# Gate and up projections: products of a block summed by TensorE onto running PSUM banks

## The chip, the cores and the metric

The kernel runs on one core of a Trainium2 chip. That core has TensorE for matrix products (PE in the profile, with its weight loads as PEld), VectorE (DVE), ScalarE (ACT), GpSimd (POOL) and the DMA queues, here those that SyncE (SP) and GpSimd issue. Each engine takes its own instructions in order and waits for others through semaphores. The metric is the time of one execution on the device in microseconds (us). Three executions of the kernel before took 2392.41, 2394.06 and 2399.23 us; their median, 2394.06 us, is the time before.

## The reference

One encoder block on a sequence of 1024 rows of width 1024, all in float32:

```
x <- LN1(alpha*x + 0.5*FFN1(x))
x <- LN2(alpha*x + W_out [attention(x) ; RG-LRU(x)])
x <- LN3(alpha*x + 0.5*FFN2(x))
swiglu(x) = (silu(x @ w_gate) * (x @ w_up)) @ w_down      # the FFN: 1024 -> 4096 -> 1024
```

Only the two products `x @ w_gate` and `x @ w_up` of both FFNs are touched by the change. Attention, the recurrence, the layer norms and `w_down` stay as they are.

## The kernel before

**Precision.** Every float32 operand is split in two parts, hi (a cast by ScalarE) and lo (the rest, a subtraction by VectorE). A float32 product is then three matmuls, hi*hi + hi*lo + lo*hi (`mm3`, L149 to L155), each with a 128x128 weight tile and 512 columns.

**Seven products for eight.** Gate and up are computed in a Strassen-Winograd scheme. `gate_up` (L276) goes over 16 pairs of 128 hidden columns; in each pair it handles two matrices, gate and up. For each matrix there are four blocks of weights (`11`, `12`, `21`, `22`; differences `t1` to `t4` of them are made by VectorE in `less`, L299) and, made once for an FFN, eight operand blocks of x (`11`, `12`, `22`, `s1` to `s4`). Seven products of 12 matmuls each (`one` to `seven`, L341 to L362) are summed to the four 128x512 results `c[0]` to `c[3]`. Each product gets a fresh PSUM bank of the eight (`banks`, L80); ScalarE copies `one` and `five` to rows `p1` and `p5`, and VectorE does all the sums: one for `two`, two for `six`, one for `three`, two for `seven`, one for `four`, seven for a matrix and each 128x512. Then ScalarE applies silu to gate, and VectorE multiplies, forms sums for the down projection and GpSimd stores the result (`finish`, L417).

**The start of an FFN.** The operand blocks of x are made while pair 0 runs. `blocks_2` (L252) transposes the rows by TensorE into PSUM, and for each of four row blocks j it makes `s1` and `22`, then, after products `one` and `two`, `s2`, `s3` and `s4`: VectorE forms the difference (L268, L270, L272), ScalarE casts hi (L244), and lo is subtracted at L245, by VectorE for `s1`, `22` and `s2`, by GpSimd for `s3` and `s4` (L271, L273). Product `six` needs `s2` of all four row blocks, so TensorE can go on with `six` only when the fourth `s2` is there. In pair 0 the products run in the order one, two, five, four, six, three, seven for gate and up in turn.

**What sets the order.** The code is written in the order above, and a scheduler in the tile framework then places each instruction on its engine's queue; tiles and pools set the waits. Weight tiles `ws` are a ring of 16, raw weights `raw` a ring of two loads of 1 MB, rows `row` a ring of eight.

**After gate and up.** `down_ffn` (L438) multiplies the stored hidden blocks with `w_down`: its operands are cast by ScalarE at L465 and subtracted by VectorE at L466, from the first matmul on. Before the second FFN stands the attention, whose last rows pass through a layer norm (L194, L204).

Of the kernel before, what the change touches and what calls it, by code (L numbers as in the profile page):

```python
# [17 lines left out]
P = 128  # L18
# [33 lines left out]
class Block:  # L52
# [26 lines left out]
    @contextmanager  # L79
    def banks(self):  # L80
        with self.pool("bank", 8, space=PSUM) as ps:
            yield lambda: ps.tile([P, H], F32, tag="b", name=self.nm("b"))
# [66 lines left out]
    def mm3(self, out, lhs, rhs, first, last):  # L149

        mm = self.nc.tensor.matmul
        (ah, al), (bh, bl) = lhs, rhs
        mm(out, ah, bh, start=first, stop=False)  # L153
        mm(out, ah, bl, start=False, stop=False)  # L154
        mm(out, al, bh, start=False, stop=last)  # L155
# [86 lines left out]
    def block_parts(self, name, j, src, eng=None):  # L242
# [9 lines left out]
    def blocks_2(self, rows, bank, tmp):  # L252
# [13 lines left out]
        for j in range(4):  # L266
# [4 lines left out]
            self.block_parts("s3", j, t21[j], nc.gpsimd)  # L271
            v.tensor_tensor(s[j], a12, s[j], ALU.subtract)  # L272
            self.block_parts("s4", j, s[j], nc.gpsimd)  # L273
            yield

    def gate_up(self, wg, wu, h_d, rows, bank, tp, wsp, aside=None):  # L276
# [9 lines left out]
        def weights(pair, n, w):  # L286
# [18 lines left out]
            if pair == 0:  # L305
                w["21"] = parts(b21)
            yield
            t1 = less(b12, b11)
            w["t1"] = parts(t1)
            if pair == 0:  # L310
                t2 = less(b22, t1)
                w["t4"] = parts(less(b21, t2))
                yield
                w["t2"] = parts(t2)
            else:
                t2 = less(b22, t1)
                w["t2"] = parts(t2)
            yield
            w["22"] = parts(b22)
            yield  # L320
            w["t3"] = parts(less(b22, b12))
            yield
            if pair:
                w["21"] = parts(b21)
                w["t4"] = parts(less(b21, t2))

        class Matrix:


            def __init__(m):  # L330
                m.w = {}
                p = self.row()
                m.p1, m.p5 = p[:, 0:H], p[:, H:]

            def product(m, n, a):
                x = bank()
                for k in range(4):
                    self.mm3(x, tuple(t[:, k, :] for t in m.w[n]), tuple(t[:, k, :] for t in A[a]), k == 0, k == 3)
                return x

            def one(m):  # L341
                nc.scalar.copy(m.p1, m.product("11", "11"))

            def two(m):
                v.tensor_tensor(m.c[0], m.product("21", "12"), m.p1, ALU.add)
# [685 lines left out]
```

## Time and profile before

| what | value |
|---|---|
| median of three executions | 2394.06 us |
| the profiled execution's own time | 2396.48 us |
| its span in the trace | 2394.8 us, so 1.7 us lie around it |
| mean granted clock of TensorE | 0.985 of full speed |
| busy in the span | PE 97%, DVE 76%, ACT 41%, POOL 16% |
| gate and up of FFN1 and of FFN2 | about 17 to 646 us and 1433 to 2064 us |

The trace is one execution. Times in its rows are us from the start of the span; the granted clock is the share of TensorE's full 2.4 GHz that the chip gave, and 0.50 is its lower level, 1.2 GHz. A busy PE is not a PE at its peak; its matmuls overlap, so the time of one in a row is longer than the step from one to the next. The same overlap, smaller, is there on VectorE and ScalarE.

### The profile page before, as it was taken

Reading aid. Unit: us, or ns where it says so; the run is one execution under the profiler, and the core shown is the slowest. Engines: PE = TensorE matmul, PEld = TensorE weight load, DVE = VectorE, ACT = ScalarE, POOL = GpSimd, SP = SyncE. Lnnn points to the kernel's source line nnn. Section 1 sums busy time; section 2 is a strip of 40 time slices with the busy share of each in tenths; the row PEclk is TensorE's granted clock in tenths of the full one; section 3 lists DMA queues with packets and bytes.
Section 4 is the critical chain, followed back from the end, with each engine's and each line's share of the span. In section 5 each row is a group of like instructions: output and inputs, shape, how many; then the busy total and the mean of one; then the engine's idle time right before and its main releaser. Section 6 shows DMA issues by size and latency. Waiting matters only on the chain.

```text
span 2394.8 us, 29276 instructions
## 1 busy us (share of the span) xinstructions
PE 2318.7 (97%) x10709; PEld 1927.6 (80%) x10709; DVE 1814.8 (76%) x3059; ACT 993.3 (41%) x1748; POOL 383.0 (16%) x461
## 2 busy tenths in 40 slices
PE   7999999999999998999999898999999999999996
PEld 5888888888888886788888777888888888888885
DVE  7877777777667878866667889776777777568879
ACT  5343333333344444544546755333333333344443
POOL 2020000000000006311134542000000000010015
PEclk8999999999999999999999998999999999999998
DMA  3333233332374442333365812332323233555342
GB/s 129 116 96 115 84 118 101 111 106 93 137 257 160 158 159 71 87 105 95 106 185 141 238 53 75 110 115 84 115 89 127 94 105 115 189 213 186 125 145 88
DMA packets 175775, 298.99 MB, mean 125 GB/s; under 512 B 8128, under 2 KB 100608, under 8 KB 175632
## 3 DMA queue, kind: packets, MB, share of 16 engines
q1 hardware_dynamic: 151984, 216.06, 28.2%
q0 software_dynamic: 23648, 81.07, 9.0%
q8 instruction: 85, 1.39, 0.3%
q14 instruction: 58, 0.48, 0.1%
HBM read 214.22 MB, written 82.87 MB: 124 GB/s over the span
## 4 chain that ended last, share of the span: by engine, by line
PE 85%; DVE 8%; issue 3%; DMA 1%; ACT 1%; POOL 1%; SPq 0%; POOLq 0%; DVEq 0%; ACTq 0%
PE b L154 17%; PE b L155 17%; PE b L153 17%; PE s L155 5%; PE s L154 5%; PE s L153 5%; PE a L155 5%; PE a L154 5%; PE a L153 5%; DVE ws L466 2%; DVE row L194 2%; PE a L851 1%; DMA raw<-in_ffn_w_gate_dram 1%; DVE st L190 1%; PE a L835 1%
## 5 line engine op out<-in xcount | busy, mean ns | idle before, releaser
L153 PE MATMUL b<-As,ws 128*128 128x512 f32 x1024 | 400.7, 392 | 8.2 <-ACT As L244 8.2
L154 PE MATMUL b<-As,ws 128*128 128x512 f32 x1024 | 400.7, 391 | 3.8 <-DVE As L245 3.8
L155 PE MATMUL b<-As,ws 128*128 128x512 f32 x1024 | 400.3, 391 | 0.0
L153 PE MATMUL b<-A,ws 128*128 128x512 f32 x768 | 299.7, 390 | 4.3 <-ACT ws L295 4.3
L154 PE MATMUL b<-A,ws 128*128 128x512 f32 x768 | 299.2, 390 | 0.0
L155 PE MATMUL b<-A,ws 128*128 128x512 f32 x768 | 299.0, 389 | 0.0
L295 ACT CAST ws<-t 128x512 fp32r<-128x512 f32 x256 | 159.5, 623 | 331.0 <-PE b L154 304.3
L465 ACT CAST ws<-raw 128x512 fp32r<-128x512 f32 x224 | 139.2, 622 | 314.8 <-PE a L155 141.3
L466 DVE TENSOR_TENSOR ws<-raw,ws 128x512 fp32r<-128x512 f32 x224 | 167.8, 749 | 120.4 <-ACT ws L465 120.2
L153 PEld LDWEIGHTS b<-As,ws 128*128 128x128 f32 x1024 | 193.3, 189 | 48.7 <-ACT As L244 8.6
L154 PEld LDWEIGHTS b<-As,ws 128*128 128x128 f32 x1024 | 193.5, 189 | 45.4 <-DVE As L245 5.2
L155 PEld LDWEIGHTS b<-As,ws 128*128 128x128 f32 x1024 | 193.5, 189 | 40.2
L295 ACT CAST ws<-raw 128x512 fp32r<-128x512 f32 x192 | 119.2, 622 | 252.1 <-PE b L154 244.5
L296 DVE TENSOR_TENSOR ws<-t,ws 128x512 fp32r<-128x512 f32 x256 | 177.9, 695 | 53.2 <-ACT ws L295 53.1
L154 PE MATMUL a<-ws,ws 128*128 128x512 f32 x512 | 202.0, 395 | 7.0 <-DVE ws L466 6.9
L153 PE MATMUL a<-ws,ws 128*128 128x512 f32 x512 | 201.4, 394 | 1.4 <-ACT ws L465 1.3
L155 PE MATMUL a<-ws,ws 128*128 128x512 f32 x512 | 201.5, 394 | 0.0
L153 PEld LDWEIGHTS b<-A,ws 128*128 128x128 f32 x768 | 144.3, 188 | 34.3 <-ACT ws L295 4.7
L296 DVE TENSOR_TENSOR ws<-raw,ws 128x512 fp32r<-128x512 f32 x192 | 136.9, 714 | 44.7 <-ACT ws L295 44.6
L429 POOL DMA_DIRECT2D h_d<-row x32 | 18.6, 581 | 937.7 <-DVE row L421 906.2
L155 PEld LDWEIGHTS b<-A,ws 128*128 128x128 f32 x768 | 144.3, 188 | 29.9
L154 PEld LDWEIGHTS b<-A,ws 128*128 128x128 f32 x768 | 144.3, 188 | 29.7
(224 smaller groups left out, 4688.7 us busy)
## 6 DMA issues: line engine op xcount, KB each, us to landing
raw<-h_d SPq DMA_DIRECT2D x56, 1024.0 KB, 5.5
h_d<-row POOLq DMA_DIRECT2D x96, 512.0 KB, 3.4
raw<-in_ffn_w_gate_dram SPq DMA_DIRECT2D x32, 1024.0 KB, 5.5
raw<-in_ffn_w_up_dram SPq DMA_DIRECT2D x32, 1024.0 KB, 5.5
wd<-in_ffn_w_down_dram SPq DMA_DIRECT2D x32, 1024.0 KB, 7.8
h_d<-row POOLq DMA_DIRECT2D x32, 256.0 KB, 4.5
raw<-in_w_in_dram SPq DMA_DIRECT2D x16, 512.0 KB, 5.2
row<-in_x_dram SPq DMA_DIRECT2D x12, 512.0 KB, 7.5
```

Of the source, the lines that this page charges most:

```text
L153: mm(out, ah, bh, start=first, stop=False)
L154: mm(out, ah, bl, start=False, stop=False)
L155: mm(out, al, bh, start=False, stop=last)
L190: v.bn_stats(st[:, j, :], a[:, j * H:(j + 1) * H])
L194: v.scalar_tensor_tensor(a, a, mv[:, 0:1], gb[0], op0=ALU.subtract, op1=ALU.mult)
L295: nc.scalar.copy(hi, src)
L296: v.tensor_tensor(lo, src, f32(hi), ALU.subtract)
L429: return nc.gpsimd.dma_start(d[:, 6], s5)
L465: nc.scalar.copy(hi, src)
L466: self.mark = v.tensor_tensor(lo, src, f32(hi), ALU.subtract)
L835: nc.tensor.transpose(pa[:, (j % 4) * P:(j % 4 + 1) * P], p[:, j * P:(j + 1) * P], self.ident)
L851: mm(pv[:, ps], vt[:, j, :], pts[h, qt][j // 4][l][:, j % 4, ps], start=j == 0 and l == 0, stop=j == last and l == 1)
```

## The change

Two of the eight PSUM banks become a pool of their own for running sums. Product `one` opens a sum bank; `six`, `seven` and `four` are added onto it by TensorE itself, and between them the bank's state is copied out: by ScalarE after `one` (`s1`) and `six` (`u`), by VectorE with the addition of `s5` after `seven` (`c[3]`), by ScalarE after `four` (`c[2]`). Product `three` is added the same way onto the bank of `five`. VectorE keeps three sums of a matrix (`two`, `seven`, `three`). `four` of a matrix is put after `one` of the next matrix (`pending`). In pair 0 each matrix keeps five sums, and `three` comes last. `s3` and `s4` get their lo part from VectorE, as the others do. The weight parts are made in the order in which the products take them. The products with silu and the multiplication work on whole rows of 1024 in place of halves.

```diff
     def banks(self):
-        with self.pool("bank", 8, space=PSUM) as ps:
+        with self.pool("bank", 6, space=PSUM) as ps, self.pool("sum", 2, space=PSUM) as xs:
+            self.sum_bank = lambda: xs.tile([P, H], F32, tag="x", name=self.nm("x"))
             yield lambda: ps.tile([P, H], F32, tag="b", name=self.nm("b"))
...
-        (eng or self.nc.vector).tensor_tensor(lo, src, f32(hi), ALU.subtract)
+        self.nc.vector.tensor_tensor(lo, src, f32(hi), ALU.subtract)
...
-            self.block_parts("s3", j, t21[j], nc.gpsimd)
+            self.block_parts("s3", j, t21[j])
             v.tensor_tensor(s[j], a12, s[j], ALU.subtract)
-            self.block_parts("s4", j, s[j], nc.gpsimd)
+            self.block_parts("s4", j, s[j])
...
             w["11"] = parts(b11)
-            if pair == 0:
-                w["21"] = parts(b21)
+            w["21"] = parts(b21)
             yield
             t1 = less(b12, b11)
-            w["t1"] = parts(t1)
             if pair == 0:
+                w["t1"] = parts(t1)
                 t2 = less(b22, t1)
                 w["t4"] = parts(less(b21, t2))
                 yield
                 w["t2"] = parts(t2)
+                yield
+                w["t3"] = parts(less(b22, b12))
+                yield
+                w["22"] = parts(b22)
             else:
                 t2 = less(b22, t1)
                 w["t2"] = parts(t2)
...
+                w["t1"] = parts(t1)
+                w["t3"] = parts(less(b22, b12))
+                w["22"] = parts(b22)
                 w["t4"] = parts(less(b21, t2))
...
-            def product(m, n, a):
-                x = bank()
+            def product(m, n, a, x=None):
+                new = x is None
+                if new:
+                    x = bank()
                 for k in range(4):
-                    self.mm3(x, tuple(t[:, k, :] for t in m.w[n]), tuple(t[:, k, :] for t in A[a]), k == 0, k == 3)
+                    self.mm3(x, tuple(t[:, k, :] for t in m.w[n]), tuple(t[:, k, :] for t in A[a]), new and k == 0, k == 3, not new)
                 return x
 
             def one(m):
-                nc.scalar.copy(m.p1, m.product("11", "11"))
+                m.sum = self.sum_bank()
...
+                nc.scalar.copy(m.s1, m.sum)
...
+            def six(m):
+                nc.scalar.copy(m.u, m.product("t2", "s2", m.sum))
 
             def five(m):
-                nc.scalar.copy(m.p5, m.product("t1", "s1"))
-
-            def six(m):
-                v.tensor_tensor(m.u, m.product("t2", "s2"), m.p1, ALU.add)
-                v.tensor_tensor(m.c[1], m.u, m.p5, ALU.add)
+                m.z = m.product("t1", "s1")
+                nc.scalar.copy(m.s5, m.z)
+
+            def seven(m):
+                v.tensor_tensor(m.c[3], m.product("t3", "s3", m.sum), m.s5, ALU.add)
 
             def three(m):
-                v.tensor_tensor(m.c[1], m.product("22", "s4"), m.c[1], ALU.add)
-
-            def seven(m):
-                v.tensor_tensor(m.u, m.product("t3", "s3"), m.u, ALU.add)
-                v.tensor_tensor(m.c[3], m.u, m.p5, ALU.add)
+                v.tensor_tensor(m.c[1], m.product("22", "s4", m.z), m.u, ALU.add)
 
             def four(m):
-                v.tensor_tensor(m.c[2], m.product("t4", "22"), m.u, ALU.add)
+                nc.scalar.copy(m.c[2], m.product("t4", "22", m.sum))
...
-                for step in ("five", "four_alone", "six", "three", "seven_four"):
+                for step in ("five", "four_alone", "six_five", "seven_four", "three_alone"):
...
-                for m in (gate, up):
-                    for step in ("one", "two", "five", "six", "three", "seven", "four"):
-                        getattr(m, step)()
-                    if m is gate:
-                        silu(gate.c)
...
+            for m in (gate, up):
+                m.one()
+                if pending:
+                    pending()
+                for step in ("two", "six", "five", "seven", "three"):
+                    getattr(m, step)()
+
+                def pending(m=m, gate=gate, g=(g0, g1), end=end, last=pair == FF // P // 2 - 1):
+                    m.four()
                     if m is gate:
-                        silu(gate.c)
+                        silu(g)
+                    elif not last:
+                        end()
+        pending()
```

The line numbers of the changed kernel are higher by 2 in this part (L245 becomes L247, L268 becomes L270, L272 becomes L274, L296 becomes L298) and by 22 in `down_ffn` (L465 becomes L487, L466 becomes L488).

**VectorE while `s2`, `s3` and `s4` of FFN1 are made.** The stretch before, from the difference for the second row block to that for the third; `As2`, `As3`, `As4` are the operand blocks, `ws` here also holds the differences, `b` are banks, `t` differences of weights.

```order
L268 TENSOR_TENSOR ws_58_251<-ws_58_251,b_90_421 128x512
L270 TENSOR_TENSOR ws_57_250<-b_90_421,ws_57_250 128x512
L296 TENSOR_TENSOR ws_95_445<-t_81_352,ws_94_444 128x512
L245 TENSOR_TENSOR As2_18_118<-ws_58_251,As2_17_117 128x4x128
L296 TENSOR_TENSOR ws_103_515<-raw_42_198,ws_102_514 128x512
L272 TENSOR_TENSOR ws_58_251<-b_91_426,ws_58_251 128x512
```

The same stretch now:

```order
L270 TENSOR_TENSOR ws_60_255<-ws_60_255,b_92_425 128x512
L272 TENSOR_TENSOR ws_59_254<-b_92_425,ws_59_254 128x512
L247 TENSOR_TENSOR As4_15_117<-ws_56_237,As4_14_116 128x4x128
L247 TENSOR_TENSOR As2_19_121<-ws_60_255,As2_18_120 128x4x128
L247 TENSOR_TENSOR As3_13_115<-ws_59_254,As3_12_114 128x4x128
L274 TENSOR_TENSOR ws_60_255<-b_93_430,ws_60_255 128x512
L298 TENSOR_TENSOR ws_95_445<-t_76_342,ws_94_444 128x512
```

The subtractions for `As3` and `As4` now stand among VectorE's, and the splits of raw weights (`raw`) have moved behind the fourth `As2`. From the first of the four differences to the fourth `As2` VectorE has 22 instructions before and 23 now in FFN1, 20 before and 22 now in FFN2.

**TensorE where FFN2 begins.** Before: the end of product `one` of gate, then the transposes of the last rows that the layer norm delivers (`row`).

```order
L153 MATMUL b_2282_12640<-A1_2237_12426,ws_2273_12622 128x512
L154 MATMUL b_2282_12640<-A1_2238_12427,ws_2273_12622 128x512
L155 MATMUL b_2282_12640<-A1_2237_12426,ws_2274_12623 128x512
L239 MATMUL b_2285_12656<-ident_73,row_1086_5578 128x128 x4
L239 MATMUL b_2286_12662<-ident_73,row_1086_5578 128x128 x4
```

Now:

```order
L157 MATMUL x_2132_12369<-A1_2085_12151,ws_2124_12352 128x512
L155 MATMUL x_2150_12469<-A1_2085_12151,ws_2128_12361 128x512
L156 MATMUL x_2150_12469<-A1_2086_12152,ws_2128_12361 128x512
L157 MATMUL x_2150_12469<-A1_2085_12151,ws_2129_12362 128x512
L155 MATMUL x_2150_12469<-A1_2085_12151,ws_2128_12361 128x512
L156 MATMUL x_2150_12469<-A1_2086_12152,ws_2128_12361 128x512
L157 MATMUL x_2150_12469<-A1_2085_12151,ws_2129_12362 128x512
L241 MATMUL b_2135_12385<-ident_73,row_934_5303 128x128 x4
```

Six matmuls of `one` of up (`x_2150`, its sum bank) have moved in front of the transposes.

**ScalarE where gate and up of FFN1 end.** Before: the last copy (`five` of up), a small cast for a later stage, and then the casts of the down projection.

```order
L342 COPY row_968_4913<-b_1015_5095 128x512
L465 CAST ws_1038_5237<-raw_1030_5225 128x512
L348 COPY row_968_4913<-b_1017_5123 128x512
L138 CAST hi_1451_7814<-gate_raw_1284 128x256
L465 CAST ws_1039_5240<-wd_1031_5227 128x512
```

Now:

```order
L354 COPY row_822_4627<-x_867_4812 128x512
L358 COPY row_823_4628<-b_869_4868 128x512
L367 COPY row_823_4628<-x_867_4812 128x512
L140 CAST hi_1299_7539<-gate_raw_1338 128x256
L487 CAST ws_887_4967<-wd_879_4954 128x512
```

The copy at L367 takes `four` of up, the very last product, and the casts of `w_down` stand behind it. On VectorE the sum of the last product (L362), which stood in front of L466, is gone.

## Rows read from the trace of the kernel before

**Rows 1.** The page: busy time, share and instructions of each engine.

```profile
PE 2318.7 (97%) x10709; PEld 1927.6 (80%) x10709; DVE 1814.8 (76%) x3059; ACT 993.3 (41%) x1748; POOL 383.0 (16%) x461
```

**Rows 2.** Busy time by stretch: length, PE, PEld, DVE, ACT, POOL, clock, DMA.

```profile
240.00:300.00 60.00, 60.00 (x267) 49.67 (x266) 43.16 (x69) 21.00 (x35) 2.71 (x4) 1.00 0.25 84
...
1260.00:1320.00 60.00, 59.22 (x367) 52.17 (x366) 47.50 (x127) 40.30 (x97) 25.52 (x48) 1.00 0.59 153
```

**Rows 3.** Timeline of PE, FFN1: start, time, instruction, idle before.

```profile
53.53 1.22 PE L153 MATMUL b<-As,ws 128*128 128x512 f32 x2 [4.91 <-ACT As L244]
56.51 0.79 PE L154 MATMUL b<-As,ws 128*128 128x512 f32 x1 [1.75 <-DVE As L245]
...
62.57 0.40 PE L154 MATMUL b<-As,ws 128*128 128x512 f32 x1
```

**Rows 4.** Timeline of DVE, FFN1.

```profile
37.44 0.68 DVE L268 TENSOR_TENSOR ws<-ws,b 128x512 f32<-128x512 f32 x1
38.04 0.68 DVE L270 TENSOR_TENSOR ws<-b,ws 128x512 f32<-128x512 f32 x1
...
42.24 1.67 DVE L296 TENSOR_TENSOR ws<-t,ws 128x512 fp32r<-128x512 f32 x1
...
54.71 1.75 DVE L245 TENSOR_TENSOR As<-ws,As 128x512 fp32r<-128x512 f32 x1
```

**Rows 5.** Timeline of POOL, FFN1.

```profile
42.07 1.30 POOL L245 TENSOR_TENSOR As<-ws,As 128x512 fp32r<-128x512 f32 x1 [0.40 <-ACT As L244]
```

**Rows 6.** Timeline of PE, start of FFN2.

```profile
1435.63 0.39 PE L155 MATMUL b<-A,ws 128*128 128x512 f32 x1
1439.68 6.22 PE L239 MATMUL b<-ident,row 128*128 128x128 f32 x32 [3.66 <-DVE row L204]
1445.66 0.48 PE L153 MATMUL b<-A,ws 128*128 128x512 f32 x1
...
1467.52 1.03 PE L239 MATMUL b<-ident,row 128*128 128x128 f32 x8
1471.83 0.95 PE L153 MATMUL b<-As,ws 128*128 128x512 f32 x2 [3.27 <-ACT As L244]
1474.81 0.79 PE L154 MATMUL b<-As,ws 128*128 128x512 f32 x1 [2.03 <-DVE As L245]
...
1479.37 0.39 PE L154 MATMUL b<-As,ws 128*128 128x512 f32 x1
```

**Rows 7.** Timeline of DVE, start of FFN2.

```profile
1457.90 0.68 DVE L268 TENSOR_TENSOR ws<-ws,b 128x512 f32<-128x512 f32 x1
...
1473.01 1.75 DVE L245 TENSOR_TENSOR As<-ws,As 128x512 fp32r<-128x512 f32 x1
```

**Rows 8.** Stretches as in group 2, where the clock was low.

```profile
52.90:63.10 10.20, 7.81 (x19) 5.71 (x20) 9.14 (x11) 3.54 (x6) 4.55 (x3) 0.53 0.66 205
1438.70:1445.50 6.80, 5.82 (x30) 5.82 (x31) 5.13 (x8) 3.23 (x7) 0.53 (x1) 0.55 0.30 119
1472.85:1479.70 6.85, 4.89 (x13) 3.90 (x14) 6.06 (x8) 2.24 (x4) 2.92 (x2) 0.55 0.74 248
```

**Rows 9.** Timeline of PE where the down projections begin, FFN1 and FFN2.

```profile
646.48 1.45 PE L153 MATMUL a<-ws,ws 128*128 128x512 f32 x4
648.03 0.50 PE L154 MATMUL a<-ws,ws 128*128 128x512 f32 x1
...
2065.49 0.50 PE L154 MATMUL a<-ws,ws 128*128 128x512 f32 x1 [1.16 <-DVE ws L466]
```

**Rows 10.** Timeline of DVE, end of gate and up in FFN2.

```profile
2064.14 0.69 DVE L362 TENSOR_TENSOR row<-b,row 128x512 f32<-128x512 f32 x1 [0.83 <-PE b L155]
```

**Rows 11.** Timeline of ACT, end of gate and up in FFN1.

```profile
635.80 0.59 ACT L348 COPY row<-b 128x512 f32<-128x512 f32 x1 [2.10 <-PE b L155]
...
641.31 0.62 ACT L465 CAST ws<-wd 128x512 fp32r<-128x512 f32 x1 [4.62 <-DMA wd<-in_ffn_w_down_dram]
```

**Rows 12.** The page: DMA issues, count, KB each, us to landing.

```profile
raw<-in_ffn_w_gate_dram SPq DMA_DIRECT2D x32, 1024.0 KB, 5.5
```

More of the change, by code (lines that the diff above doesn't have):

```diff
@@ L147, in split_ws, with mm3 @@
         return hi, lo
-    def mm3(self, out, lhs, rhs, first, last):
+    def mm3(self, out, lhs, rhs, first, last, goes_on=False):
         mm = self.nc.tensor.matmul
         (ah, al), (bh, bl) = lhs, rhs
-        mm(out, ah, bh, start=first, stop=False)
-        mm(out, ah, bl, start=False, stop=False)
-        mm(out, al, bh, start=False, stop=last)
+        mm(out, ah, bh, start=first, stop=False, skip_group_check=goes_on)
+        mm(out, ah, bl, start=False, stop=False, skip_group_check=goes_on)
+        mm(out, al, bh, start=False, stop=last, skip_group_check=goes_on)
     def open_xT(self, pool, half):
@@ L339, in product @@
                 return x
             def one(m):
-                nc.scalar.copy(m.p1, m.product("11", "11"))
+                m.sum = self.sum_bank()
+                for k in range(4):
+                    self.mm3(m.sum, tuple(t[:, k, :] for t in m.w["11"]), tuple(t[:, k, :] for t in A["11"]), k == 0, k == 3)
+                nc.scalar.copy(m.s1, m.sum)
             def two(m):
-                v.tensor_tensor(m.c[0], m.product("21", "12"), m.p1, ALU.add)
+                v.tensor_tensor(m.c[0], m.product("21", "12"), m.s1, ALU.add)
@@ L364, in four_alone, with six_five, three_alone @@
             def four_alone(m):
                 nc.scalar.copy(m.c[2], m.product("t4", "22"))
+            def six_five(m):
+                m.six()
+                v.tensor_tensor(m.c[1], m.u, m.s5, ALU.add)
             def seven_four(m):
                 m.seven()
-                v.tensor_tensor(m.c[2], m.c[2], m.u, ALU.add)
+                v.tensor_tensor(m.c[2], m.c[2], m.sum, ALU.add)
+            def three_alone(m):
+                v.tensor_tensor(m.c[1], m.product("22", "s4"), m.c[1], ALU.add)
@@ L373, in silu, with halves @@
                 nc.scalar.activation(t, t, AF.Silu)
+        def halves(r):
+            return r[:, 0:H], r[:, H:]
+        pending = None
         for pair in range(FF // P // 2):
             if pair == 0:
[L377 to L385 removed]
@@ L386, in gate_up @@
-            h = h0, h1
-            gate.u, up.u = us
-            gate.c = [g[:, k * H:(k + 1) * H] for g in (g0, g1) for k in range(2)]
-            up.c = [h[n][:, m * H:(m + 1) * H] for m in range(2) for n in range(2)]
-            w = [weights(pair, n, m.w) for n, m in enumerate((gate, up))]
+                g0, h0, first, fifth, uu, g1, h1, u = (self.row() for _ in range(8))
+                homes = list(zip(halves(first), halves(uu), halves(fifth)))
+                gate, up = Matrix((g0, g1), *homes[0]), Matrix((h0, h1), *homes[1])
+            else:
+                g0, g1, uu, h0, h1, u = (self.row() for _ in range(6))
+                gate, up = (Matrix(r, r[1][:, 0:H], x, r[0][:, H:]) for r, x in zip(((g0, g1), (h0, h1)), halves(uu)))
@@ L391, in gate_up, with end @@
+            def end(pair=pair, finish=finish):
+                store = finish()
+                if aside is not None and pair == 2:
+                    with self.tc.issue_after(store.ins):
+                        aside()
             if pair == 0:
```

66 lines of the change are left out of this document (24 added, 42 removed).

## The prediction

> **What bounds the kernel now.** I read the page's busy shares first. VectorE is at 76%, so a change that takes sums from it looks promising; but TensorE is at 97% [rows 1]. The next view is the busy time by stretch. In the middle of gate and up TensorE is busy for the whole 60 us, issues 267 matmuls, one every 0.225 us, and holds the full clock [rows 2]; VectorE has 17 us to spare in that stretch and ScalarE 39. The stretches from 120 to 600 us and from 1500 to 2040 us read alike. There nothing but fewer matmuls could help, and the change leaves their number as it is. The reader should look for time only where TensorE stands still: the start of each FFN, and the step to the down projection.
>
> The timeline of TensorE shows the start of FFN1. After the transposes it waits 4.91 us for ScalarE's cast of the fourth `s2`, issues two matmuls, and waits 1.75 us more for VectorE's subtraction of it [rows 3]. So the chain is VectorE's, from the first difference at 37.44 us to the subtraction that starts at 54.71 and takes 1.75 [rows 4]: 19.02 us for 22 instructions. Undisturbed, VectorE starts the next instruction 0.60 us after the last, with 0.68 us for one [rows 4]; 22 would take 13.3 us. The missing 5.7 us sit in instructions like the one at 42.24 us, which takes 1.67 us while GpSimd's subtraction for `s3` or `s4` runs beside it for 1.30 us [rows 4, 5]; six of the 22 are stretched so. After the wait TensorE's clock is low: the mean is 0.53 of full speed from 52.9 to 63.1 us [rows 8].
>
> FFN2 begins with a wait of 3.66 us for the layer norm's last row, then 32 transposes at 0.55 of the clock, then the same two waits for the fourth `s2`, of 3.27 and 2.03 us, and again 0.55 of the clock [rows 6, 8].
>
> **The change part by part.**
>
> *Sums on TensorE's banks, from pair 1 on.* VectorE loses four sums in each of 30 matrices of an FFN, 240 in all, and half of its multiplications become double ones; at 0.60 us a sum that is 144 us of VectorE's time. ScalarE gets two more copies a matrix, 120 of about 0.59 us [rows 11], 71 us. TensorE issues the same 12 matmuls a product, 12 x 0.225 = 2.7 us. I take 0 for all of it, since TensorE is the engine that never waits here [rows 2]. What is new is that `six`, `seven`, `four` and `three` wait for the copy of their bank. The copy starts close behind the product's end and takes 0.59 us [rows 11], and a whole product of 2.7 us lies between: about 1.9 us in hand. If the cover goes, each microsecond of lateness is a microsecond of TensorE's (a rival, below).
>
> *`s3` and `s4` without GpSimd.* In FFN1 VectorE now has 23 instructions from the first difference to the fourth `As2`, of which six are subtractions that GpSimd did; the two splits of raw weights that stood among them come later. With GpSimd silent I price all at the undisturbed step: 22 x 0.60 + 0.68 = 13.9 us, against 19.0, so -5.1. In FFN2 the chain runs from 1457.90 to 1473.01 + 1.75, 16.9 us for 20 instructions [rows 7]; 22 now take 21 x 0.60 + 0.68 = 13.3, so -3.6. Bounds: nothing gained, if the stretching has another cause; and no more than the waits that there are, 6.7 us in FFN1 and 5.3 in FFN2 [rows 3, 6]. So 1.6 to 1.7 us of waiting should stay in each. The Trainium skill (Perfetto Trace Analysis, Optimizing Scalar/DVE Operations) speaks against this edit on one side: where VectorE is saturated, as it is in these 19 us, handing work to ScalarE or even GpSimd may make sense. The same passage adds that GpSimd and VectorE share a read port into SBUF, so that it may not help. By the first half the chains would grow by the instructions added and the sum would lose its two largest terms; the instruction that takes 1.67 us beside GpSimd's speaks for the second half.
>
> *The clock in the ramps.* From 56.51 to 62.57 us TensorE issued 14 matmuls [rows 3], 6.06 us where 14 x 0.225 = 3.15 are enough: 2.9 us. From 1474.81 to 1479.37 it issued 11 [rows 6], 4.56 against 2.5: 2.1 us. With waits half as long as before I expect no fall, hence -2.9 and -2.1. Bounds: 0 if the clock falls all the same.
>
> *Start of FFN2.* Six matmuls of `one` of up now stand before the transposes and fill 6 x 0.225 = 1.35 us of the wait for the layer norm. That wait is then broken in two, since gate's `one` must also wait until its sum bank is free of the attention's last tile; the end of both is set by the layer norm, so this costs nothing. The 32 transposes took 1445.66 - 1439.68 = 5.98 us; eight at full clock take 1.03 at most [rows 6], so 32 take 4.1: -1.9 if the clock holds, 0 if not. In sum -3.25.
>
> *The step to the down projection.* Before, VectorE's sum of the last product stood in front of its subtraction for `w_down` [rows 10]; TensorE lost 1.16 us there in FFN2, and in FFN1 1.55 - 4 x 0.225 = 0.65 [rows 9]. Now the last product's copy stands on ScalarE, and the casts of `w_down` are queued behind it: copy (0.5 us step), the small cast in FFN1 (about 0.3), cast 0.62 [rows 11], then the matmul, with the 0.17 us by which a matmul of 0.39 us outlasts its step [rows 6]: 1.6 us and, with the subtraction behind, 1.8 in FFN2. I take +1.0 and +0.7. Bounds: 0 to +1.2 each.
>
> *First pair after the ramp.* ScalarE has casts and copies bunched there, and the trace of before has no such row. Bounds 0 and one cast plus one copy, 1.2 us [rows 11]; nearest is a part of one, 0.4 for each FFN: +0.8. The raw weights of pair 0 are read later (the split of block `22` comes last), so pair 1's loads start some 6 us later; a load lands in 5.5 us [rows 12] and six products of 2.7 us stand before it is needed, so I cost that at nothing, with about 3 us in hand.
>
> *Sum* for the profiled execution: -5.1 - 3.6 - 2.9 - 2.1 - 3.25 + 1.7 + 0.8 = -14.5 us, so 2396.5 - 14.5 = 2382.0. That execution stood 2.4 us above the median of the three; I forecast the median to move alike: 2379.6, rounded 2380.
>
> **The rivals.**
>
> *The clock falls anyway* in one or both ramps, or at the transposes. For it: waits of about 2 us remain, and 3.27 us were enough before. Against: what remains is about half of it. All three clock terms gone: 6.9 us back, 2386.5; one or two of them: 2382 to 2385.
>
> *No relief of VectorE.* If the long instructions are not GpSimd's doing, a chain of 23 instructions takes 0.86 us for each as before, and the ramps get 0.9 and 1.7 us longer with the clock as low as now: -3.25 + 2.6 + 2.5 = +1.9, so 2396. Against it stands that a subtraction with a bank as input, at 38.04, and those before GpSimd starts keep 0.68 us [rows 4, 5].
>
> *The re-used banks become the bound*, the slower side. On ScalarE a copy stands behind casts that wait for weight tiles which TensorE still holds. Where such a cast waits for the product between, the copy comes one cast and one copy after that product's end, 0.62 + 0.59 + 0.2 = 1.4 us of stall. Once in each pair, 30 times, that is +42 us, so 2422; from 11 such stalls on the gain is gone. For it: in gate and up ScalarE has waits of 2.10 us on TensorE in its queue [rows 11]. Against: it is busy 21 of 60 us [rows 2], and in the new order the cast ahead of a copy waits for no later product than the copy does. The Trainium skill (TensorE: Matmul & The Clock Gate, A second HAM failure mode: psum-queue depth-cycling) makes it worse: small idle times between groups of matmuls that cycle through banks can make the clock swing between its levels. Here a stretch of attention with 0.8 us of such gaps keeps 1.00 [rows 2], so the trace doesn't bear that out so far.
>
> **How the numbers follow.** My forecast, 2376 to 2384, has 0.62; the clock falling anyway 0.20; no relief 0.08; the banks as the bound 0.05; the rest, such as a late load of weights, 0.05. About 0.3%, 7 us, is what a measurement of this kernel can tell from no change, so faster means under 2386.9. The forecast and nearly all of the clock's case lie there: 0.80. No relief and what remains of the clock's case and the rest make 0.14 for the same; the banks and a little of the rest 0.06 for slower. The low end is 2373: both new costs absent, 2.5, and half of the waits that I leave in the ramps, 1.7 each, gone too, with 2 us of spread. The high end is 2390: no clock term and the step and first pair at their upper bounds.
>
> **What would show it.** Right: no `s3` or `s4` instruction on GpSimd, and each VectorE instruction from the first difference to the fourth `As2` at 0.60 us step; waits before `six` of about 2 us in sum; clock 1.00 from 30 to 600 us; a wait of about 1.6 us for ScalarE's cast at the first down-projection matmul; VectorE near 69% with TensorE's 267 matmuls per 60 us unchanged. Wrong: a PE wait on a copy or on VectorE's `seven` in gate and up, fewer than 266 matmuls in a stretch there, or a low clock after a ramp.

## The result and the profile after

| | before | changed |
|---|---|---|
| median of the executions (us) | 2395.0 of 4 | 2383.31 of 4 |
| lowest to highest | 2392.41 to 2399.23 | 2382.39 to 2387.98 |
| the profiled execution | 2396.48 | 2387.98 |

The ratio is 0.9949 with a 95% interval of 0.9934 to 0.9963: faster, by 11.7 us in the medians. The forecast was 2380, with 2373 to 2390 as its range. The profiled execution of the changed kernel is the longest of its four, so a second trace of the same kernel (2384.17 us) stands beside it below.

The page of the changed kernel, as in [rows 1]; VectorE is at 70% and PE at 97% as before:

```profile
PE 2315.0 (97%) x10709; PEld 1922.8 (81%) x10709; DVE 1668.3 (70%) x2763; ACT 1042.8 (44%) x1808; POOL 360.4 (15%) x445
```

Busy time by stretch of the changed kernel (length, PE, PEld, DVE, ACT, POOL, clock, DMA), to be read beside [rows 2, 8]: the middle of gate and up, the ramp of FFN1, and the two places of FFN2 where the clock was low.

```profile
240.00:300.00 60.00, 60.00 (x267) 49.67 (x266) 34.96 (x51) 23.42 (x40) 2.71 (x4) 1.00 0.26 85
50.00:53.40 3.40, 3.37 (x9) 2.24 (x8) 3.40 (x6) 1.83 (x3) 0.00 (x0) 0.56 0.02 5
1436.20:1443.00 6.80, 5.68 (x42) 5.05 (x41) 6.50 (x12) 2.77 (x6) 1.11 (x2) 1.00 0.39 157
1463.50:1470.00 6.50, 4.99 (x25) 3.72 (x24) 6.50 (x12) 3.92 (x7) 0.00 (x0) 1.00 0.01 3
```

The middle still has 267 matmuls in 60 us with VectorE at 35 us instead of 43. In FFN2 the clock no longer falls. In FFN1 it does, for one short stretch of some 3.4 us instead of ten.

The timeline of PE in the changed kernel, FFN1, against [rows 3]: one wait of 2.28 us where there were 4.91 and 1.75.

```profile
49.45 1.13 PE L155 MATMUL x<-As,ws 128*128 128x512 f32 x2 [2.28 <-ACT As L246]
```

The timeline of VectorE in the changed kernel, FFN1, against [rows 4]:

```profile
36.64 0.68 DVE L270 TENSOR_TENSOR ws<-ws,b 128x512 f32<-128x512 f32 x1
37.23 0.68 DVE L272 TENSOR_TENSOR ws<-b,ws 128x512 f32<-128x512 f32 x1
...
41.46 1.89 DVE L247 TENSOR_TENSOR As<-ws,As 128x512 fp32r<-128x512 f32 x3
...
48.66 1.89 DVE L247 TENSOR_TENSOR As<-ws,As 128x512 fp32r<-128x512 f32 x3
```

No instruction is stretched: three in a row take 1.89 us. From the first difference to the end of the fourth `As2` it is 48.66 + 1.89 - 36.64 = 13.9 us for 23 instructions.

The timeline of PE in the changed kernel, start of FFN2, against [rows 6]:

```profile
1433.82 0.47 PE L155 MATMUL x<-A,ws 128*128 128x512 f32 x1 [1.03 <-DVE row L221]
1439.28 3.69 PE L241 MATMUL b<-ident,row 128*128 128x128 f32 x32 [1.11 <-DVE row L206]
...
1465.60 0.73 PE L155 MATMUL x<-As,ws 128*128 128x512 f32 x2 [1.04 <-ACT As L246]
1466.81 0.50 PE L156 MATMUL x<-As,ws 128*128 128x512 f32 x1 [0.47 <-DVE As L247]
```

The 32 transposes take 3.69 us instead of 6.22, and the waits for `s2` 1.04 and 0.47 instead of 3.27 and 2.03.

The timelines of ScalarE and then of PE in the changed kernel where the down projection of FFN1 begins, against [rows 9, 11]: the copy of the last product stands ahead of the casts, and PE waits for a cast.

```profile
639.66 0.59 ACT L367 COPY row<-x 128x512 f32<-128x512 f32 x1 [7.57 <-PE x L157]
...
640.45 0.62 ACT L487 CAST ws<-wd 128x512 fp32r<-128x512 f32 x1
```

```profile
641.12 1.20 PE L155 MATMUL a<-ws,ws 128*128 128x512 f32 x4 [1.50 <-ACT ws L487]
```

Both kernels issue 10709 matmuls, so the start of a matmul of the same number can be compared between traces. The table gives how much longer (+) or shorter (-) each stretch is in the changed kernel, with the bounds in the time of before; the last row goes to the end of the span.

| stretch of before, us | forecast | first trace | second trace |
|---|---|---|---|
| 0 to 45, ahead of the wait in FFN1 | none | -1.46 | -1.31 |
| 45 to 97, ramp and first pair of FFN1 | -5.1 - 2.9 + 0.4 = -7.6 | -5.56 | -5.64 |
| 97 to 640, gate and up | 0 | 0.00 | +0.15 |
| 640 to 660, step to down | +1.0 | +0.97 | +0.97 |
| 660 to 1425, code not changed | 0 | +5.54 | +1.51 |
| 1425 to 1446, entry of FFN2 | -3.25 | -3.22 | -3.21 |
| 1446 to 1492, ramp of FFN2 | -3.6 - 2.1 = -5.7 | -6.17 | -6.19 |
| 1492 to 1520, first pair | +0.4 | +0.54 | +0.54 |
| 1520 to 2050, gate and up | 0 | 0.00 | -0.01 |
| 2050 to 2078, step to down | +0.7 | +0.52 | +0.52 |
| 2078 to the end, code not changed | 0 | +0.34 | +0.35 |

The stretches that the change touches agree between the two traces within 0.15 us. What lies in code that it doesn't touch differs from execution to execution: in the first trace the attention lost 5.5 us. Some 3.2 us of it fall between 1350 and 1370 us. The waits of PE from 1345 to 1365 us in that trace show a load that came late there, with the mean clock at 0.83 (columns: us in total, times, longest):

```profile
PE s L837 <- DMA kh<-k_d: 2.5, 1, 2.5
```

The start of FFN1 is shorter in both traces, which nothing in the forecast had. The timeline of PE ahead of the first weights, in the kernel before and then in the changed one:

```profile
4.61 3.52 PE L239 MATMUL b<-ident,row 128*128 128x128 f32 x16 [4.61 <-DMA row<-in_x_dram]
8.76 1.10 PE L239 MATMUL b<-ident,row 128*128 128x128 f32 x8 [0.64 <-DMA row<-in_x_dram]
11.31 1.97 PE L239 MATMUL b<-ident,row 128*128 128x128 f32 x8 [1.45 <-DMA row<-in_x_dram]
17.54 0.80 PE L153 MATMUL b<-A,ws 128*128 128x512 f32 x1 [4.26 <-ACT ws L295]
```

```profile
4.77 4.89 PE L241 MATMUL b<-ident,row 128*128 128x128 f32 x24 [4.77 <-DMA row<-in_x_dram]
11.22 2.37 PE L241 MATMUL b<-ident,row 128*128 128x128 f32 x20 [1.56 <-DVE A L247]
17.55 0.50 PE L155 MATMUL x<-A,ws 128*128 128x512 f32 x1 [3.95 <-ACT ws L297]
```

The first weights come at the same time, but 44 transposes instead of 32 stand in front of them. Twelve transposes at a step of 0.11 us are about 1.3 us, an estimate, that no longer lie behind them.

### The profile page after: what moved, and what is told of

The parts are those of the page before. It is cut to its first block, busy times and chain, and to the rows that moved or that the text cites. A ratio compares the mean times of both kernels' runs of the same rounds, so it can differ in the third digit from the quotient of the medians.

```text
span 2386.3 us, 29020 instructions
## 1 busy us (share of the span) xinstructions
PE 2315.0 (97%) x10709; PEld 1922.8 (81%) x10709; DVE 1668.3 (70%) x2763; ACT 1042.8 (44%) x1808; POOL 360.4 (15%) x445
## 5 line engine op out<-in xcount | busy, mean ns | idle before, releaser
L487 ACT CAST ws<-raw 128x512 fp32r<-128x512 f32 x224 | 139.4, 622 | 301.0 <-PE a L157 129.1
L488 DVE TENSOR_TENSOR ws<-raw,ws 128x512 fp32r<-128x512 f32 x224 | 166.3, 742 | 115.1 <-ACT ws L487 114.6
L413 POOL DMA_DIRECT2D h_d<-row x96 | 68.4, 716 | 1159.6 <-DVE row L407 1120.0
L298 DVE TENSOR_TENSOR ws<-raw,ws 128x512 fp32r<-128x512 f32 x192 | 133.7, 698 | 144.2 <-ACT ws L297 140.7
L298 DVE TENSOR_TENSOR ws<-t,ws 128x512 fp32r<-128x512 f32 x256 | 175.5, 686 | 70.4 <-ACT ws L297 68.5
L155 PE MATMUL x<-As,ws 128*128 128x512 f32 x512 | 199.8, 391 | 3.3 <-ACT As L246 3.3
L156 PE MATMUL x<-As,ws 128*128 128x512 f32 x512 | 200.0, 391 | 0.5 <-DVE As L247 0.5
L155 PE MATMUL b<-As,ws 128*128 128x512 f32 x512 | 199.6, 390 | 0.4 <-ACT row L358 0.4
L157 PE MATMUL x<-As,ws 128*128 128x512 f32 x512 | 199.7, 390 | 0.0
L157 PE MATMUL b<-As,ws 128*128 128x512 f32 x512 | 199.3, 389 | 0.0
L156 PE MATMUL b<-As,ws 128*128 128x512 f32 x512 | 199.3, 389 | 0.0
L155 PE MATMUL x<-A,ws 128*128 128x512 f32 x496 | 193.8, 391 | 5.0 <-ACT ws L297 3.9
L157 PE MATMUL x<-A,ws 128*128 128x512 f32 x496 | 193.6, 390 | 0.0
L156 PE MATMUL x<-A,ws 128*128 128x512 f32 x496 | 193.4, 390 | 0.0
L155 PE MATMUL s<-ws,ws 128*128 128x512 f32 x384 | 149.4, 389 | 0.0
L156 PE MATMUL s<-ws,ws 128*128 128x512 f32 x384 | 149.4, 389 | 0.0
L157 PE MATMUL s<-ws,ws 128*128 128x512 f32 x384 | 149.4, 389 | 0.0
```

Of the source, the lines that this page charges most:

```text
L155: mm(out, ah, bh, start=first, stop=False, skip_group_check=goes_on)
L156: mm(out, ah, bl, start=False, stop=False, skip_group_check=goes_on)
L157: mm(out, al, bh, start=False, stop=last, skip_group_check=goes_on)
L298: v.tensor_tensor(lo, src, f32(hi), ALU.subtract)
L413: nc.gpsimd.dma_start(d[:, 2 * n:2 * n + 2], t.rearrange("p (r t) -> p r t", r=2))
L488: self.mark = v.tensor_tensor(lo, src, f32(hi), ALU.subtract)
```

## The experiments

My theory A was that the gain is made in the two ramps, and that the steady state is worth nothing. The rivals were that the relief of VectorE in all pairs carries it (B), and that VectorE without GpSimd has too much to do in the first pair, so that `s3` and `s4` alone only move the wait (C).

**One half undone: GpSimd again for `s3` and `s4`.**

```
-            self.block_parts("s3", j, t21[j])
+            self.block_parts("s3", j, t21[j], nc.gpsimd)    # and s4
```

> The changed kernel with one part undone: the subtractions that build the low parts of s3 and s4 are GpSimd's again; PE still sums on running banks and VectorE still has three sums per matrix. Theory A (the gain is made in the two ramps, by VectorE's chain going at 0.6 us a step once GpSimd is out of it): the wait before the last s2 product in the first FFN is 6 to 8 us again instead of 2.28, the one in the second FFN comes back as well, VectorE's subtractions beside GpSimd take over 1.5 us, the clock falls there again; 2391 to 2397 us, that is most or all of the gain gone. Rival B (the gain comes from the sums that VectorE lost in all 64 matrices): 2383 to 2385, no change against the changed kernel.

Measured: 2392.88 us (11 executions), ratio to before 0.9980 to 0.9998. Of 11.7 us 2.1 are left. The timeline of PE in FFN1 of this kernel:

```profile
52.32 1.22 PE L155 MATMUL x<-As,ws 128*128 128x512 f32 x2 [4.20 <-ACT As L246]
55.30 0.79 PE L156 MATMUL x<-As,ws 128*128 128x512 f32 x1 [1.76 <-DVE As L247]
```

VectorE and then GpSimd in the same stretch of it:

```profile
42.87 1.78 DVE L298 TENSOR_TENSOR ws<-t,ws 128x512 fp32r<-128x512 f32 x1
...
46.27 0.68 DVE L270 TENSOR_TENSOR ws<-ws,b 128x512 f32<-128x512 f32 x1
...
53.50 1.75 DVE L247 TENSOR_TENSOR As<-ws,As 128x512 fp32r<-128x512 f32 x1
```

```profile
42.48 3.31 POOL L247 TENSOR_TENSOR As<-ws,As 128x512 fp32r<-128x512 f32 x2 [1.11 <-ACT As L246]
45.97 1.53 POOL L247 TENSOR_TENSOR As<-ws,As 128x512 fp32r<-128x512 f32 x1 [0.18 <-ACT As L246]
...
53.38 1.31 POOL L247 TENSOR_TENSOR As<-ws,As 128x512 fp32r<-128x512 f32 x1 [0.36 <-ACT As L246]
```

Both waits are back, with the long instructions, although this kernel keeps all the sums that PE took over; in FFN2 they are 4.92 and 1.75 us. B falls. The entry of FFN2 keeps its gain here (-3.2 us from 1425 to 1446), so that belongs to the other half.

**The other half left out: `s3` and `s4` on VectorE in the kernel before.**

```
-            self.block_parts("s3", j, t21[j], nc.gpsimd)    # and s4
+            self.block_parts("s3", j, t21[j])
```

> The kernel before with one part of the change alone: s3 and s4 by VectorE, the seven products still drained one by one with seven sums per matrix on VectorE. Theory A1 (GpSimd's sharing with VectorE is the whole cost): most of the gain is there, 2384 to 2387 us, and no PE wait over 3 us up to 80 us. Rival C (without GpSimd VectorE has more to do in the first pair than the time allows, so the wait is only moved): the wait before the last s2 product shrinks from about 8 us to under 3, but PE waits 6 to 7 us for weights made by VectorE or ScalarE around 70 to 80 us; 2392 to 2396 us, within 0.2% of before. I hold C at 0.6.

Measured: 2399.66 us (11 executions), ratio 1.0009 to 1.0030: slower than before by 4.7 us. The timeline of PE in FFN1 of this kernel:

```profile
50.42 0.73 PE L153 MATMUL b<-As,ws 128*128 128x512 f32 x2 [1.62 <-ACT As L244]
51.58 0.50 PE L154 MATMUL b<-As,ws 128*128 128x512 f32 x1 [0.42 <-DVE As L245]
...
77.91 0.80 PE L153 MATMUL b<-A,ws 128*128 128x512 f32 x1 [5.85 <-ACT ws L295]
```

ScalarE in it, just ahead:

```profile
76.72 0.62 ACT L295 CAST ws<-t 128x512 fp32r<-128x512 f32 x1 [4.04 <-DVE t L301]
```

Its busy time by stretch, with VectorE (third) without a pause:

```profile
70.00:80.00 10.00, 3.96 (x14) 2.45 (x13) 10.00 (x18) 3.61 (x7) 2.17 (x3) 0.80 0.40 149
```

C holds, and goes further than I had put it: the wait for `s2` shrinks as hoped, and PE then waits longer than before for weights of pair 1, whose differences VectorE makes last. One half alone is +4.7 us, the other alone -2.1, both together -11.7.

**Where the two halves need each other, from both sides.** First `s3` and `s4` on VectorE, with VectorE's sums cut in the first two pairs only (the edit shortened, in words where it says so):

```
 def six(m):
+    if pair == 1: nc.scalar.copy(m.u, x)        # instead of the sum of u
+    if pair >= 2: the sum into c[1]
 def seven(m):  # pairs 0 and 1: one sum instead of two
 def four(m):   # pair 1: nc.scalar.copy instead of the sum
```

> The kernel before with s3 and s4 by VectorE, as in the run that had only this, and with VectorE's sums in the first two pairs cut to the number that the changed kernel has there (five per matrix in pair 0, three in pair 1, where ScalarE copies two products instead); what those sums would have added is left out, so the outputs differ; the other 14 pairs keep seven sums per matrix, and nothing is summed on PE's banks. Theory A (the two parts of the change need each other only in the first two pairs: without the sums that the change takes from VectorE there, s3 and s4 make VectorE late for the weights of pair 1): PE's wait of 5.85 us for weights near 78 us shrinks to under 3 and so does the one in the second FFN; 2386 to 2391 us, against 2399.7 with s3 and s4 alone. Rival (the wait comes from the order in which the weights are made, or the sums of the later pairs matter): it stays at 5 us or more, 2396 to 2400.

Measured: 2385.43 us (8 executions), ratio 0.9954 to 0.9976, 14 us under the run with `s3` and `s4` alone. The timeline of PE in FFN1:

```profile
72.43 0.50 PE L153 MATMUL b<-A,ws 128*128 128x512 f32 x1 [1.19 <-ACT ws L295]
75.61 0.50 PE L155 MATMUL b<-A,ws 128*128 128x512 f32 x1 [1.52 <-DVE ws L296]
```

5.85 us have become 1.19 and 1.52; at the same place in FFN2 waits of 3.4 and 1.2 us have become none. Fourteen of sixteen pairs still have all their sums on VectorE, and 9.8 us of gain are there.

Then the changed kernel with the load of before put back in those two pairs:

```
+                m.again = int(pair < 2)
...
-                v.tensor_tensor(m.c[0], m.product("21", "12"), m.s1, ALU.add)
+                x = m.product("21", "12")
+                for _ in range(1 + m.again):               # seven likewise, three 1 + 2 * m.again
+                    v.tensor_tensor(m.c[0], x, m.s1, ALU.add)
```

> The changed kernel with VectorE's load of the kernel before put back in the first two pairs alone: the sums of two and seven made twice in pair 0 (seven sums per matrix instead of five), and those of two and seven twice and that of three three times in pair 1 (seven instead of three); the same values again. Theory A: PE waits for weights or sums near 70 to 95 us in the first FFN and at the same place in the second, 1.5 to 5 us in each; 2386 to 2394 us. Rival (that load is hidden in the first pairs too, and the gain that the two parts have together comes from the new order of the weights): 2382 to 2385.

Measured: 2389.84 us (8 executions), ratio 0.9967 to 0.9987: 6 us of the gain gone, as A has it in time, though not where I expected it. The timeline of PE in FFN1:

```profile
49.76 0.73 PE L155 MATMUL x<-As,ws 128*128 128x512 f32 x2 [2.88 <-ACT As L246]
51.51 0.64 PE L156 MATMUL x<-As,ws 128*128 128x512 f32 x1 [1.02 <-DVE As L247]
```

Here the extra sums stand in the chain to `s2` itself, whose waits grow from 2.28 to 3.90 us (in FFN2 from 1.51 to 2.70), and near 70 to 95 us there is nothing over 0.7. VectorE is full from 36 to 54 us, so sums added ahead of the fourth `s2` are paid for.

This run also shows that a third part of the change counts. VectorE has as many sums in the first two pairs here as in the kernel with `s3` and `s4` alone. That kernel waits 5.85 us for weights of pair 1 and is 4.7 us slower than before; this one has no such wait and is 5.4 us faster. Its waits for `s2` are 1.9 us longer, which leaves VectorE that much more time, but not 5.85. So the rest of the change, its new order of the weights and products and its running banks, hides that wait as well, and the rival is right on this point. No run takes the new order by itself, so the share of the weights' order stays open.

**VectorE's load back in all later pairs.** The same edit with `m.again = int(pair > 0)`.

> The changed kernel with VectorE's load put back from the second pair on: of every matrix the sums of two and seven are made twice and that of three three times (the same values written again), four more instructions of 0.6 us in each of 60 matrices, 144 us of VectorE work in all; the first pairs stay as they are. Theory A (the steady state is bound by PE, and VectorE's relief there is worth nothing): 2383 to 2385 us, no change; VectorE busy 76% instead of 70%. Rival B (relief of VectorE in the steady state carries the gain): 2388 to 2395, toward the kernel before.

Measured: 2385.45 us (5 executions), ratio 0.9938 to 0.9963: no change clear of noise. The trace has two waits for these sums and copies in gate and up of FFN1, 0.44 us at 87 and 0.63 at 175 us, and none in FFN2 behind its first pair. The page shows VectorE at 76% as in the kernel before:

```profile
PE 2314.7 (97%) x10709; PEld 1922.5 (81%) x10709; DVE 1803.7 (76%) x3003; ACT 1038.7 (44%) x1808; POOL 359.2 (15%) x445
```

**How much the re-used bank has in hand.** The timelines of ScalarE and then of PE in the changed kernel show it for one matrix: the copy after `six`, and the start of `seven`.

```profile
305.40 0.58 ACT L354 COPY row<-x 128x512 f32<-128x512 f32 x1
```

```profile
307.62 0.39 PE L155 MATMUL x<-As,ws 128*128 128x512 f32 x1
```

The copy ends 1.64 us before `seven` needs the bank. Then the copy is made again, two or five times more:

```
-                nc.scalar.copy(m.u, m.product("t2", "s2", m.sum))
+                m.product("t2", "s2", m.sum)
+                for _ in range(1 + 2 * (pair > 0)):      # then 1 + 5 * (pair > 0)
+                    nc.scalar.copy(m.u, m.sum)
```

> The changed kernel with ScalarE's copy of the running bank after six made three times instead of once, from the second pair on (the same values again): the bank comes free 1.0 us later for seven. Theory G (a product of another bank, 2.7 us long, lies between six and seven, so the copy has about 1.6 us to spare): 2383 to 2387 us, PE hardly waits in the steady state. Rival H (the re-used bank is already close to the bound): a wait of 0.5 to 1.0 us in each of 60 matrices, 2413 to 2445.

Measured: 2387.12 us (6 executions), ratio 0.9957 to 0.9980, about 3 us over the changed kernel. The waits of PE from 70 to 130 us:

```profile
PE x L155 <- DVE row L363: 2.4, 1, 2.4
```

That is one wait in pair 1, where ScalarE and VectorE are still behind; one of 0.75 us follows at 180 us. From 300 to 640 us there is no loss.

> The same with six copies instead of one: the bank comes free 2.6 us later than in the changed kernel. Theory G (1.6 us to spare) wants PE to wait at seven of every matrix from the second pair on, some 0.3 to 1.0 us each in 60 matrices, more if the clock falls: 2403 to 2445 us. Rival (ScalarE has longer to spare, or seven waits for something else already): no change, 2383 to 2388.

Measured: 2403.39 us (5 executions), ratio 1.0025 to 1.0052. The middle of gate and up:

```profile
240.00:300.00 60.00, 59.97 (x262) 48.49 (x261) 34.44 (x51) 31.41 (x53) 2.70 (x4) 1.00 0.25 84
```

262 matmuls instead of 267: from 120 to 640 us the kernel loses 10.3 us over about 27 matrices of 19.06 us, 0.38 us each, with the clock at 1.00. G's time is met at the low end of its range, but not by its mechanism. The timelines of ScalarE and then of PE in one matrix:

```profile
309.95 2.44 ACT L356 COPY row<-x 128x512 f32<-128x512 f32 x4
313.27 0.60 ACT L360 COPY row<-b 128x512 f32<-128x512 f32 x1
313.75 0.61 ACT L356 COPY row<-x 128x512 f32<-128x512 f32 x1
```

```profile
313.93 0.50 PE L155 MATMUL b<-As,ws 128*128 128x512 f32 x1
314.73 0.40 PE L155 MATMUL x<-As,ws 128*128 128x512 f32 x1
```

The copies last until 314.36, and `seven` (`x<-As`) starts at 314.73: the scheduler has put seven matmuls of another product and three of `three` in front of it. What PE stands still for is `three` at 313.93, which adds onto the bank of `five`; the copy of that bank ends at 313.87, queued among the repeated ones. So two more copies fit behind the product and five don't, but 0.38 us is what is left after the queue was filled otherwise, and no measure of `seven`'s own wait.

**The changed kernel once more.**

> The changed kernel itself once more, beside the others of this series, to have more executions of it and a second trace. Theory A: 2382 to 2385 us again; in the trace PE's waits at the ramps, at the steps to the down projections and the low clock in the first FFN stand as before, and what the first trace lost in the attention in between (about 5 us, in code that the change doesn't touch) does not come back. Rival: that loss belongs to the change, and this trace has it too.

Measured: 2384.17 us (5 executions, 2381.18 to 2389.90). The second trace is in the table above; 4.0 of the first one's 5.5 us in the attention are not in it.

**The step to the down projection.**

```
-                nc.scalar.copy(m.c[2], m.product("t4", "22", m.sum))
+                (v.tensor_copy if last else nc.scalar.copy)(m.c[2], m.product("t4", "22", m.sum))
```

> The changed kernel with the copy of the very last product of the gate/up loop (up's four, last pair, in both FFNs) made by VectorE instead of ScalarE, so that ScalarE's eight casts for the down projection don't stand behind it. Theory D (the 1.50 us that PE waits for ScalarE's cast at the step to the down projection is that copy's place in ScalarE's order): the casts are done before the last product ends, PE's wait there falls from 1.5 to 0.7 us or less in both FFNs, VectorE's subtractions become the releaser, 1.0 to 2.0 us less in all: 2381 to 2383. Rival E (the casts wait for their loads or buffers anyway, or VectorE's copy takes the place of ScalarE's): the wait stays at 1.3 us or more and the time is the changed kernel's.

Measured: 2383.18 us (5 executions), ratio 0.9932 to 0.9957. The timeline of PE at the two steps:

```profile
640.93 0.96 PE L155 MATMUL a<-ws,ws 128*128 128x512 f32 x3 [0.56 <-DVE row L367]
...
2052.16 0.50 PE L156 MATMUL a<-ws,ws 128*128 128x512 f32 x1 [1.16 <-DVE ws L488]
```

In FFN1 the wait is 0.56 instead of 1.50. In FFN2 the waits of 1.19 and 0.23 have become one of 1.16, not under 0.7 and the same as in the kernel before [rows 9]. By the numbers of the matmuls both steps cost 0.0 instead of 0.97 and 0.52. 1.5 us are too few for the medians to show, so the gain stands in the trace alone.

**What is left in the ramp of FFN1.** On top of the last edit, the low parts of `s3` and `s4` after the last `s2`, and then also the last block's transposes ahead of up's `four`:

```
             v.tensor_tensor(t21[j], a11, t21[j], ALU.subtract)
-            self.block_parts("s3", j, t21[j])
             v.tensor_tensor(s[j], a12, s[j], ALU.subtract)
-            self.block_parts("s4", j, s[j])
+            if j == 3:
+                for i in range(4): self.block_parts("s3", i, t21[i])
+                for i in range(4): self.block_parts("s4", i, s[i])
...
                         next(blocks, None)
+                        if step == "four_alone":
+                            next(blocks, None)
```

> The changed kernel with up's last product copied by VectorE (as in the run before), the transposes of the last block put ahead of up's four, and the low parts of s3 and s4 made only after the last s2. Theory F (the 2.28 us that PE waits for the last s2 in the first FFN is the order of VectorE's work, with the low parts of s3 and s4 ahead of it): that wait shrinks to under 1 us, the clock doesn't fall there, the second FFN's 1.04 goes too; 2 to 4 us less than the changed kernel with both ends, 2379 to 2382. Rival (VectorE works without a break from 36 to 54 us, so a wait removed there comes back at the next product): the waits up to 60 us still sum to about 2 us, 2382 to 2384.

> The fastest kernel so far (2380.4 us) without its earlier transposes: up's last product copied by VectorE, and the low parts of s3 and s4 made after the last s2. Theory F1 (VectorE's order sets the wait for the last s2 in the first FFN): that wait is under 1 us and the clock doesn't fall, 2379.5 to 2381.5. Theory F2 (the transposes of the last block, behind up's four, set it): the wait stays at 1.5 us or more, and the clock falls or not as the wait is long; 2381.5 to 2383.5.

Measured: 2380.40 us (2378.95 to 2382.96), ratio 0.9927 to 0.9952, with both; 2380.90 us, ratio 0.9930 to 0.9953, without the transposes. The timeline of PE in FFN1 with both edits:

```profile
48.22 0.50 PE L156 MATMUL x<-As,ws 128*128 128x512 f32 x1 [0.40 <-DVE As L247]
...
54.89 0.50 PE L155 MATMUL x<-As,ws 128*128 128x512 f32 x1 [1.39 <-ACT ws L300]
```

Its busy time by stretch:

```profile
45.00:66.00 21.00, 19.22 (x82) 14.75 (x81) 19.06 (x32) 11.15 (x18) 0.00 (x0) 1.00 0.32 101
```

And the timeline of PE without the transposes:

```profile
49.16 0.73 PE L155 MATMUL x<-As,ws 128*128 128x512 f32 x2 [1.50 <-ACT As L246]
```

The rival was half right: with both, the wait for `s2` goes to 0.40 and one of 1.39 us for a weight's cast comes some 7 us later, so the sum falls only from 2.28 to 1.79. In FFN2 a wait of 1.19 us for a weight's cast stands in place of the two for `s2`. The clock is 1.00 from 45 to 66 us in both kernels; that the shorter waits keep it up is not shown, as the last section tells. Without the transposes the wait is 1.50 (1.03 in FFN2), as F2 has it, and the time is F1's. The two times can't be told apart. With all three edits the median is 3.8 us under the changed kernel beside which it ran, and its slowest execution is below that one's median; the two intervals against before still overlap a little.

## Why the prediction was right, and where not

- *Steady state 0*: right. PE keeps 267 matmuls per 60 us, and 144 us of VectorE's work put back in the later pairs cost nothing that the times can tell.
- *The chain of VectorE*: right in size. 13.9 us forecast in FFN1 and 13.9 measured; in FFN2 13.3 and 13.5 (1453.30 to 1466.76). The cause is shown by the run with GpSimd put back. The wait before it shrank by 4.4 us in FFN1 and not by 5.1, because TensorE came to it 1.46 us earlier and VectorE's first difference only 0.80 us earlier (36.64 against 37.44).
- *But not right in what it was credited to.* I gave the chain's gain to `s3` and `s4` alone and priced the sums at 0 everywhere. The first edit by itself costs 4.7 us, since VectorE is then late for pair 1. The sums have their worth in the first two pairs, as the runs with the sums cut and put back in these two pairs show from both sides: 14 us without the rest of the change, some 6 with it. The new order I had priced only where FFN2 begins and at the raw weights of pair 0; by itself or with the running banks it hides the wait for the weights of pair 1 too. The total came out because all of it was changed together; as a sum of separate prices it was wrong.
- *Clock*: -2.1 and -1.9 in FFN2 came as forecast (ramp -6.2 in all, transposes 3.69 us). In FFN1 the clock fell once more, for 3.4 us at half: the rival "the clock falls anyway" in one of its three places. The 14 matmuls behind the fourth `s2` took 4.43 us, where 6.06 stood before and 3.15 were forecast: -1.6 instead of -2.9. That is 1.3 us of the 2.0 that this stretch is short of the forecast, and the largest miss among the terms; most of the rest is the wait above.
- *Entry of FFN2 -3.25*: measured -3.2, and it is there with GpSimd put back too. *Steps +1.0 and +0.7*: +0.97 and +0.52. *First pair +0.4 each*: +0.54 in FFN2, in FFN1 the same from 80 to 97 us; the only wait there that the trace names, on a copy, is 0.2.
- *Missed*: the start of FFN1 is 1.3 to 1.5 us shorter (0.5 to 2.8 in all the kernels with sum banks, not shorter in the two without). All ten traces with sum banks have 44 transposes ahead of the first weights, the three without have 32; the clock behind them adds to the spread: up to 45 us it was low for 6.1 us in the kernel with 0.5 and not at all in those with 2.2 and 2.8, nor in one with 1.2. Which edit moves the transposes was not tried.
- *The re-used banks*: no wait over 0.2 us on them in the changed kernel. I worked out 1.9 us in hand and the trace has 1.64, as a cast stands ahead of the copy; two more copies cost nothing in the steady state. The Trainium skill's rule that cycling through banks can make the clock swing (TensorE: Matmul & The Clock Gate, A second HAM failure mode: psum-queue depth-cycling) is not borne out: with five more copies the clock is 1.00 from 120 to 600 and from 1520 to 2030 us, even with a stall in each matrix.
- *The median*: 2383.3 and not 2380. The touched stretches sum to -12.9 in either trace, apart from the start, and with it to -14.4 and -14.2, against -14.5 forecast. That this is so close is luck: the start, which I had not priced, makes up for most of what the clock and the wait in FFN1 fell short. The second trace spent 1.9 us more than the one of before in code that nobody touched, and the first 5.9, where, from 660 to 1425 us, the twelve traces of the other kernels and executions spread from -3.0 to +5.5 us against that one. A single trace of before was a good base for the terms and a weak one for the total.

## What to carry over

Where an engine is full only in a ramp, price the edits of that ramp together: count every instruction that the engine must do until the next engine is served, in the order in which it will do them, not each edit's own. Work taken from a busy engine in the steady state is worth nothing while another engine is the bound, yet the same edit can pay in the two iterations after the ramp. Price the clock of a ramp both ways: the 14 matmuls behind the fourth `s2` took 4.43 us with the fall and 3.30 without it (in the last kernel, without the earlier transposes), and waits of 2 us in sum came with either.

## What the runs showed of the hardware

- VectorE beside GpSimd: with both inputs in SBUF (`ws<-t,ws`) 1.78 us, with one from a PSUM bank (`ws<-ws,b`, at 46.27 beside GpSimd's 45.97) 0.68. The Trainium skill (SBUF — State Buffer, Who interferes with whom) says just this: outside its two-port modes a VectorE instruction with at most one SBUF input does not contend with GpSimd. The trace agrees.
- Waits of PE at the ramp and the clock behind them, 45 to 66 us: 2.28 us, low for 3.4 us in both traces of the changed kernel; 1.50 and 0.42, not low; 1.62 and 0.42 in the kernel with `s3` and `s4` alone, low, and 1.61 and 0.42 in its variant with fewer sums, not low. In FFN2 of the kernel with `s3` and `s4` alone the clock was low after 1.16 and 0.42 (1472.1 to 1475.5 us), in the changed kernel not after 1.04 and 0.47. The same waits went either way, so the length of the wait alone does not tell the outcome here.
